# Transposing the exponentials of an attention block in two DMAs, high parts and low parts apart

## The chip, the cores and the metric

The kernel runs on one core of one Trainium2 chip. A core has a matrix engine (TensorE, in the profile PE, its weight loads PEld), a vector engine (VectorE, DVE), an activation engine (ScalarE, ACT), GpSimd (POOL), SyncE (SP, which here issues the DMAs) and 16 DMA engines that move what SP issues. The metric is the time of one execution on the device in microseconds (us); less is better.

## What is computed

Two request groups of 1024 rows and 1024 columns each go through the same two layers. Each layer is a hybrid block; the attention is the part that matters here.

```
h = rmsnorm(x) * (1 + scale) + shift          # from the conditioning vector
u = h @ w_in                                  # pool | q | k | v | rg | gate columns
y_pool, y_rg = pooling mixer, gated linear recurrence
q, k = rope(rmsnorm(q)), rope(rmsnorm(k))     # 8 query heads, 2 key heads, 64 wide
s = q @ k.T * scale;  p = softmax(s);  y_attn = p @ v
x = x + gate * rmsnorm((concat(y_pool, y_attn, y_rg) * silu(u_gate)) @ w_out)
```

## The kernel before

There are four passes (two layers times two groups, `n` = 0 to 3), one after the other with overlaps. Products are made of float16 numbers in pairs: an operand is split into a high part (rounded to float16) and a low part (the rest), and hi*hi, hi*lo and lo*hi are added in PSUM.

**The attention of one pass** (`attn_gen`, from line 1212) is 64 units, one for 128 query rows of one head. A unit goes through seven steps:

1. TensorE makes the scores of 128 rows against 1024 keys, four matmuls of 512 columns, into two PSUM banks.
2. VectorE finds the row maximum (`mx`).
3. ScalarE makes the exponentials (`p`), either in place in PSUM or into a buffer in SBUF, which frees the two banks sooner.
4. ScalarE rounds them to float16: the high part, `hh[:, 0, :]`.
5. GpSimd (exponentials in SBUF) or VectorE (in PSUM) subtracts it from the exponentials: the low part, `hh[:, 1, :]`.
6. One DMA transpose, 128 partitions by 2048 columns, turns both parts into `pT` (16 blocks of 128 by 128). The call is `dma_t` (line 478), and the profile has it under line 479.
7. TensorE multiplies `pT` with the values, 24 matmuls of 64 columns: 8 with the high parts against the high values, 8 with the low parts, and 8 with the high parts against the low values.

**What orders the work.** The whole program is laid out when it is built. Every piece of work is a generator that says what it needs, and the class `Order` (from line 84) keeps a clock of its own for each engine, for the DMA queue and for each tile, and takes the generator that can go on first, by rank where several can. Each engine then runs its instructions in the order so written; an instruction whose input isn't there holds all those behind it on its engine. All DMAs are issued by SP, in one order: the transposes, the loads of weights and rows, and the stores. `TUNE` (line 27) has some forty numbers for each pass: ranks of the pieces, how many units may be in flight (`nfly`), how many pairs of PSUM banks may hold scores (`np`), slacks in the choice of engine. `Order.dma` (line 242) books a transpose in that clock; `PARTS` and `keys` let the clock follow the pieces of a tile apart.

Buffers `p`, `hh` and `pT` come from a share of `nfly` + 2 slots of SBUF (`"u"`).

The end of a unit before, from line 1231 on:

```
hh = slot([P, 2, 1024], F16, "hh", "u")
...
act(hh[:, 0, :], p, AF.Copy)
...
tt(hh[:, 1, :], p, hh[:, 0, :], ALU.subtract)
free(p)
yield need("S", [hh], u=1)
pT = slot([P, 16, P], F16, "pT", "u")
dma_t(pT, hh.rearrange("p a s -> p (a s)"))
free(hh)
```

Of the kernel before, what the change touches and what calls it, by code (L numbers as in the profile page):

```python
# [10 lines left out]
F16 = mybir.dt.float16  # L11
# [5 lines left out]
P = 128  # L17
D = 1024
# [9 lines left out]


TUNE = [  # L30
    dict(h=-9.8, tab=-61.5, rgw=-62.8, qw=11.3, q=39.5, main=39.6, v=-93.1, rgt=6.2, attn=13.3,
         wprep=16.5, wo=39.7, side=108.5, gate=1.45, ysc=107.7, ysp=100.7, w=68.8, work=8, ds=3, nfly=8,
         s0=4, pace=(4, 61), wos=8, deep=3, f_major=5, spare=0, qkeep=1, wkeep=7, wokeep=0, slack=2.19,
         hslack=2.0, margin=0.33, P=0.6, A=1.22, D=1.02, G=1.25, S=1.3, X=2.99, nb=4, np=2, wopen=3,
         spill=2, sslack=0.0),
    dict(h=-88.0, tab=-138.2, rgw=-45.0, qw=-61.2, q=-181.1, main=65.6, v=-122.9, rgt=23.6, attn=-14.4,
         wprep=107.1, wo=85.3, side=97.8, gate=1.86, ysc=66.7, ysp=108.8, w=79.4, work=8, ds=2, nfly=5,
         s0=0, pace=(14, 64), wos=10, deep=3, f_major=6, spare=1, qkeep=5, wkeep=2, wokeep=9, slack=3.75,
         hslack=3.82, margin=0, P=0.07, A=1.29, D=0.36, G=1.39, S=1.66, X=1.74, nb=4, np=3, wopen=4,
         spill=2, sslack=0.0),  # L40
    dict(h=-56.5, tab=-120.9, rgw=-43.7, qw=-41.0, q=-17.5, main=-3.7, v=-95.2, rgt=51.8, attn=-16.0,
         wprep=71.4, wo=90.7, side=118.4, gate=0.1, ysc=142.5, ysp=110.2, w=62.9, work=6, ds=2, nfly=6,
         s0=3, pace=(15, 38), wos=9, deep=2, f_major=1, spare=4, qkeep=2, wkeep=0, wokeep=1, slack=2.33,
         hslack=2.48, margin=0.36, P=2.36, A=1.02, D=0.83, G=0.625, S=0.35, X=1.72, nb=6, np=2, wopen=3,
         spill=2, sslack=0),
    dict(h=-38.8, tab=-7.4, rgw=44.8, qw=-59.1, q=43.0, main=31.5, v=86.0, rgt=62.7, attn=36.1,
         wprep=226.9, wo=-31.1, side=118.1, gate=0.51, ysc=119.3, ysp=81.6, w=57.1, work=10, ds=3, nfly=5,
         s0=5, pace=(0, 64), wos=9, deep=4, f_major=3, spare=1, qkeep=5, wkeep=1, wokeep=0, slack=2.26,
         hslack=2.98, margin=0.87, P=0.28, A=0.15, D=0.45, G=0.9, S=1.99, X=0, nb=4, np=3, wopen=4,
         spill=2, sslack=0.28),  # L50
]
START = dict(x=(6, 16), xr=(-53.8009657012761, 1.4378218455368525), h=11.7, qw=-116.3, qw2=-141.6, qwa=9,
             prt=7, crow=4, prow=2, ada=95.9, keep=0)
LAYER = [
    dict(fly=6, keep=3, wfly=4, wfrom=(0, 0), wrank=15.7, ada=-17.0, akeep=5),
    dict(fly=3, keep=2, wfly=1, wfrom=(1, 1), wrank=163.6, ada=69.7, akeep=8),
]
LAT = {
# [6 lines left out]
PARTS = {}  # L65
# [8 lines left out]
def keys(ap):  # L74

    name = ap.name
    if name[:4] != "psum":
        step = PARTS.get(name)
        return (f"{name}/{ap.offset // step}",) if step else (name,)
    c = ap.offset % 4096  # L80
    return [f"psum/{i}" for i in range(c // 512, (c + sum(s * (n - 1) for s, n in list(ap.ap)[1:])) // 512 + 1)]
# [7 lines left out]
class Order:  # L89
# [18 lines left out]
    def spawn(self, rank, gen):  # L108
        insort(self.live, [rank, gen, None], key=lambda z: z[0])
# [132 lines left out]
    def dma(self, dur, outs, ins, hold, tail, e="S"):  # L242
        t = max(self.now, self.free_at[e], self.lanes[self.issued % 8])
        for ap in ins:
            t = max(t, self.there(ap.name, "S"))
        for ap in outs:
            t = max(t, self.last.get(ap.name, 0.0))
        x = max(t + 1.3, self.free_at["X"])
        self.free_at["X"] = x + dur
        self.free_at[e] = max(t + hold, x + dur - (1.8 if hold > 1.0 else 9.0))  # L250
        t = x + dur + tail
        self.lanes[self.issued % 8] = t
        self.issued += 1
        for ap in (*ins, *outs):
            self.last[ap.name] = max(self.last.get(ap.name, 0.0), t)
        for ap in outs:
            self.ready.setdefault(ap.name, {})["X"] = t

    def mark(self, name, *tiles):

# [40 lines left out]
def need(eng="", on=(), cond=None, keep=0, **bufs):  # L301
    return [eng, on, bufs, keep, cond, None]


def cols(ap):
    n = 1
    for x in ap.shape[1:]:
        n *= x
    return n
# [3 lines left out]
def tile_hymba_encoder(  # L313
# [43 lines left out]
    od = Order({"s": NS, "H": 2, "h": NH})  # L357
    free, spawn = od.free, od.spawn
# [3 lines left out]
    def nm(s):  # L362
        uid[0] += 1
        return f"{s}_{uid[0]}"

    def slot(shape, dt, name, pool="s"):
        return od.take(pool, sp.tile(shape, dt, tag="s", name=nm(name)))

    def half(shape, dt, name):
        return od.take("h", hp_.tile(shape, dt, tag="h", name=nm(name)))  # L370

    def small(n, name, dt=F32):
        return sm.tile([P, n], dt, tag="m", name=nm(name))

    def bank(name):
        i = od.bank(1)
        return banks[:, 512 * i:512 * i + 512]
# [99 lines left out]

    def dma_t(out, in_):
        nc.sync.dma_start_transpose(out=out, in_=in_)  # L479
        od.dma(2.55 * cols(in_) / 2048, [out], [in_], 1.8, 0.6)  # L480

    def soonest(*choice):

# [89 lines left out]
    G = {}  # L573

    def rows_dma(l, pr):
        for i, (r0, n, src) in enumerate((
# [9 lines left out]
        )):  # L586
            yield need("S", cond=lambda: l or G.get("adas", 0) >= START["prow"] + i)
            dma(pr[r0:r0 + n, :], src)

    def load_rows(l):  # L590
        yield need("S", h=1)
        pr = half([64, P], F32, "prow")
        yield from rows_dma(l, pr)
        yield need("P", [pr], b=1, cond=lambda: l or G.get("adas", 0) >= START["prt"])
        ps = bank("prT")
# [34 lines left out]
    def silu_c():  # L630
        yield need("S", h=1, cond=lambda: G.get("adas", 0) >= START["crow"])
        cr = half([16, P], F32, "crow")
# [196 lines left out]
    def h0_gen(rank):  # L829
# [4 lines left out]
        def load(j):  # L834
            yield need(s=8, cond=lambda: G.get("adas", 0) >= START["x"][j])
            xs = []
# [69 lines left out]
        spawn(-99.9, columns(0))  # L906
        spawn(START["xr"][0], load(0))
        spawn(START["xr"][1], load(1))
        yield need(cond=lambda: ("hgb", 0) in G)
# [250 lines left out]
    V16 = {}  # L1160
# [49 lines left out]
    def attn_gen(n, rank):  # L1210
        SUM, O, DONE = {}, {}, {}
        fly = [0]

        def unit(i, S):
            hp, q, e, t = UNITS[i]
            h = 2 * hp + e
            yield need("D", [S])
            mx = small(1, "mx")
            red(mx, S, ALU.max, negate=True)
            sc = G["qksc", n]  # L1220
            ts(mx, mx, sc, PSHIFT, ALU.mult, ALU.add)
            if (hp, q) not in SUM:
                SUM[hp, q] = sums.tile([P, 8], F32, tag="s8", name=nm("sum"))
            yield need("A", [mx], u=1)

            out = od.pairs >= TUNE[n]["spill"] and od.claims["u"] >= 2
            p = slot([P, 1024], F32, "p", "u") if out else S
            act(p, S, AF.Exp, bias=mx, scale=sc, accum=SUM[hp, q][:, 2 * t + e:2 * t + e + 1])
            if out:
                free(S)  # L1230
            hh = slot([P, 2, 1024], F16, "hh", "u")
            yield need("A", [p])
            act(hh[:, 0, :], p, AF.Copy)
            yield need("D", [hh])
            if out:
                sub_any(hh[:, 1, :], p, hh[:, 0, :])
            else:
                tt(hh[:, 1, :], p, hh[:, 0, :], ALU.subtract)
            free(p)
            yield need("S", [hh], u=1)  # L1240
            pT = slot([P, 16, P], F16, "pT", "u")
            dma_t(pT, hh.rearrange("p a s -> p (a s)"))
            free(hh)
            if (hp, q) not in O:
                yield need(b=1)
                if (hp, q) not in O:
                    O[hp, q] = bank("O")
                    DONE[hp, q] = 0
            yield need("P", [pT, V16[n, hp // 2]])
            v = V16[n, hp // 2]  # L1250
            c = (2 * t + e) * HD
            mms(O[hp, q][:, c:c + HD], [(pT[:, 8 * (a == 1) + st, :], v[:, st, HD * (a == 2):HD * (a == 2) + HD]) for a in range(3) for st in range(8)],
                True, True, (pT, v))
            free(pT)
            fly[0] -= 1
            if G["unit", n] == NU:
                held = sum(x == "u" for x in od.home.values())
                od.claims["u"] = max(0, min(od.claims["u"], fly[0] + 2 - held))
            DONE[hp, q] += 1
            if DONE[hp, q] == 8:  # L1260
                yield from join(hp, q)
# [29 lines left out]
        nfly = TUNE[n]["nfly"]  # L1291
        yield need(s=nfly + 2, cond=lambda: G.get(("rgc", n)) == 1 and G["side", n] >= TUNE[n]["s0"])
        od.claim("u", nfly + 2, True)
        for i in range(NU):
            hp, q, e, t = UNITS[i]
            h = 2 * hp + e
# [7 lines left out]
            S = bank2("S")  # L1304
# [523 lines left out]
```

## Time and profile before

| what | value |
|---|---|
| median of 3 runs | 1880.79 us (1875.88 to 1883.11) |
| the profiled execution, its own time | 1876.88 us |
| its span from first to last instruction | 1875.1 us |
| mean granted clock of TensorE, share of full speed | 0.975 |
| TensorE busy in matmuls | 1712.4 us (91% of the span) |
| VectorE, ScalarE, GpSimd busy | 1280.2, 1140.2, 760.5 us |
| bytes moved by DMAs | 323.58 MB |

The median says what the kernel takes. The profiled execution is one more run with the profiler on; its rows explain one another and its own time, so that sums are made against 1876.88 us and then held against the median.

Read the busy shares with care: an engine that is busy for 91% of the span leaves 9% for waits, and what can be gained at first is only in those waits. The profile names what ended each wait. SP has no busy time in the table, since all that it does is to wait and to issue; its rows (SPq) are instructions whose duration is the time that SP spent on the issue. A landing is the time from the start of that instruction until the last of its data is there.

### The profile page before, as it was taken

What the parts mean: (1) busy time and instruction counts of PE and PEld (TensorE: products, weight loads), DVE (VectorE), ACT (ScalarE), POOL (GpSimd) and SP (SyncE); (2) the same over time, 40 slices, a digit from 0 to 9 for tenths busy, and PEclk for the clock granted to TensorE, in tenths of its full rate; (3) what the DMA queues carried; (4) which work ended last, traced back from release to release, by engine and by line L of the source; (5) the groups of instructions that cost most, each with busy time, mean ns of one, the idle gap of its engine ahead of it and who ended that gap; (6) DMA issues with size and microseconds to landing.
All of it is one profiled execution on the core that took longest, in us unless ns stands there. A gap on an engine that the chain in (4) does not pass through costs nothing.

```text
span 1875.1 us, 35819 instructions
## 1 busy us (share of the span) xinstructions
PE 1712.4 (91%) x14267; PEld 990.7 (53%) x14267; DVE 1280.2 (68%) x2327; ACT 1140.2 (61%) x1767; POOL 760.5 (41%) x602
## 2 busy tenths in 40 slices
PE   5799899988999989999799998898789999999898
PEld 2564555544555546555456646455445755555543
DVE  4796987786345889567646689886843577866741
ACT  3665677776415667677642376678753256888721
POOL 2731452353431244234343226346643214655432
PEclk7899999999999989999899999999999999999999
DMA  9674499999365559999843446799984322999943
GB/s 345 201 208 153 99 191 233 178 214 252 136 225 191 131 137 206 168 194 214 232 147 135 101 102 128 145 251 191 179 234 151 102 68 41 178 201 195 198 133 116
DMA packets 672592, 323.58 MB, mean 173 GB/s; under 512 B 597880, under 2 KB 628776, under 8 KB 672424
## 3 DMA queue, kind: packets, MB, share of 16 engines
q1 hardware_dynamic: 672424, 321.29, 74.1%
q8 instruction: 111, 1.82, 0.4%
q14 instruction: 57, 0.47, 0.1%
HBM read 128.28 MB, written 46.15 MB: 93 GB/s over the span
## 4 chain that ended last, share of the span: by engine, by line
PE 32%; DVE 11%; issue 5%; ACT 4%; DMA 4%; POOL 4%; SPq 1%; POOLq 0%; ACTq 0%; DVEq 0%
PE psum L395 31%; POOL hh L423 4%; DMA pT<-hh 3%; DVE mx L459 3%; ACT p L410 2%; DVE psum L423 1%; ACT hh L410 1%; PE psum L403 1%; DVE y L450 1%; DMA xt<-xmid 1%; DVE sq L423 1%; SPq L479 1%; DVE hh L423 1%; DVE pdf L450 0%; DVE qss L459 0%
## 5 line engine op out<-in xcount | busy, mean ns | idle before, releaser
L423 POOL TENSOR_TENSOR hh<-p,hh 128x1024 f16<-128x1024 f32 x187 | 406.8, 2179 | 416.2 <-ACT hh L410 382.2
L395 PE MATMUL psum<-hT,w 128*128 128x512 f16 x2304 | 538.0, 381 | 5.8 <-ACT w L410 3.4
L459 DVE TENSOR_REDUCE mx<-psum 128x1 f32<-128x1024 f32 x256 | 312.0, 1219 | 94.2 <-PE psum L395 76.0
L395 PEld LDWEIGHTS <-w 128*128 128x128 f16 x2304 | 221.7, 99 | 273.6 <-issue 26.9
L395 PE MATMUL psum<-wo,y 128*128 128x512 f16 x1536 | 346.6, 382 | 3.7 <-DVE y L442 1.6
L395 PE MATMUL psum<-qkT,qkT 128*128 128x512 f16 x1024 | 265.7, 385 | 39.3 <-ACT p L410 24.7
L410 ACT ACTIVATE p<-psum,mx,qksc 128x1024 f32<-128x1024 f32 x187 | 224.1, 1199 | 106.8 <-DVE mx L444 63.9
L395 PE MATMUL psum<-w,hT 128*128 128x256 f16 x2304 | 273.5, 276 | 9.0 <-POOL hT L423 6.4
L395 PEld LDWEIGHTS <-pT 128*128 128x128 f16 x6144 | 212.8, 99 | 122.7 <-DMA pT<-hh 85.1
L395 PE MATMUL psum<-v,pT 128*128 128x64 f16 x6144 | 225.8, 194 | 54.8 <-DMA pT<-hh 54.6
L395 PEld LDWEIGHTS <-hT 128*128 128x128 f16 x2304 | 226.5, 100 | 60.3 <-issue 17.5
L395 PEld LDWEIGHTS <-y 128*128 128x128 f16 x1536 | 149.5, 99 | 175.4 <-issue 5.6
L410 ACT ACTIVATE hh<-p 128x1024 f16<-128x1024 f32 x187 | 196.5, 1053 | 4.9
L395 PEld LDWEIGHTS <-qkT 128*128 128x128 f16 x1024 | 93.0, 99 | 133.7 <-issue 58.0
L450 DVE SCALAR_TENSOR_TENSOR ot<-psum,ors,gp 128x512 f32<-128x512 f32 x64 | 45.1, 745 | 154.8 <-POOL ors L423 154.8
L410 ACT ACTIVATE junk<-psum 128x512 bf16<-128x512 f32 x64 | 38.2, 596 | 181.8 <-PE psum L395 170.4
L423 DVE TENSOR_TENSOR hh<-psum,hh 128x1024 f16<-128x1024 f32 x69 | 84.1, 1218 | 31.7 <-ACT hh L410 31.5
L423 POOL TENSOR_TENSOR ws<-ws,neghalf 128x1 f32<-128x1 f32 x46 | 28.5, 635 | 186.5 <-DVE ws L442 185.6
L423 POOL TENSOR_TENSOR ot<-ot,xres 128x1024 f32<-128x1024 f32 x31 | 73.2, 2361 | 66.7 <-DVE ot L450 32.5
L410 ACT ACTIVATE psum<-psum,mx,qksc 128x1024 f32<-128x1024 f32 x69 | 80.8, 1170 | 24.1 <-DVE mx L444 19.4
L410 ACT ACTIVATE hh<-psum 128x1024 f16<-128x1024 f32 x69 | 70.3, 1019 | 1.7
L423 POOL TENSOR_TENSOR qrs<-qrs,neghalf 128x8 f32<-128x8 f32 (+1 forms) x48 | 68.7, 1432 | 4.0
(219 smaller groups left out, 2073.1 us busy)
## 6 DMA issues: line engine op xcount, KB each, us to landing
adaw<-in_ada_w_dram SPq DMA_DIRECT2D x48, 512.0 KB, 6.1
wraw<-in_w_in_dram SPq DMA_DIRECT2D x36, 512.0 KB, 6.4
wd<-w SPq DMA_DIRECT2D x36, 512.0 KB, 3.3
w<-wd SPq DMA_DIRECT2D x36, 512.0 KB, 4.7
wo<-wd SPq DMA_DIRECT2D x32, 512.0 KB, 6.2
woraw<-in_w_out_dram SPq DMA_DIRECT2D x16, 512.0 KB, 4.6
wd<-wo SPq DMA_DIRECT2D x16, 512.0 KB, 4.1
xmid<-ot SPq DMA_DIRECT2D x16, 512.0 KB
```

The lines of the kernel that those rows point to most:

```text
L395: nc.tensor.matmul(out[:, :m], lhsT, rhs, start=start and i == 0, stop=stop and i == len(pairs) - 1)
L403: nc.tensor.transpose(out, in_, idn)
L410: nc.scalar.activation(out=out, in_=in_, func=func, **kw)
L423: eng.tensor_tensor(out=out, in0=a, in1=b, op=op)
L450: nc.vector.scalar_tensor_tensor(out=out, in0=a, scalar=s, in1=b, op0=op0, op1=op1)
L459: nc.vector.tensor_reduce(out=out, in_=a, op=op, **{"axis": AX.X, **kw})
L479: nc.sync.dma_start_transpose(out=out, in_=in_)
```

## The change

A unit now issues two transposes of 1024 columns instead of one of 2048. The first (`turn_hi`) is issued when the high part is there, and its slot for `pT` is taken then; the second follows when the low part is there, into the second half of the same `pT`. The matmuls with the values wait for both. `Order.dma` keeps the two halves of `hh` and `pT` apart and books each transpose at half the length. 26 numbers in the tables `TUNE`, `START` and `LAYER` are others (among them `np` of pass 0, 3 instead of 2, and ranks of the pieces `side`, `wo` and `attn`); of these one line of pass 0 and one of pass 3 stand here.

```diff
-         wprep=16.5, wo=39.7, side=108.5, gate=1.45, ysc=107.7, ysp=100.7, w=68.8, work=8, ds=3, nfly=8,
+         wprep=16.5, wo=43.7, side=158.1, gate=1.45, ysc=107.7, ysp=100.7, w=68.8, work=8, ds=3, nfly=8,
...
-         s0=5, pace=(0, 64), wos=9, deep=4, f_major=3, spare=1, qkeep=5, wkeep=1, wokeep=0, slack=2.26,
+         s0=5, pace=(0, 64), wos=9, deep=5, f_major=2, spare=1, qkeep=5, wkeep=1, wokeep=0, slack=2.26,
...
     def dma_t(out, in_):
         nc.sync.dma_start_transpose(out=out, in_=in_)
-        od.dma(2.55 * cols(in_) / 2048, [out], [in_], 1.8, 0.6)
+        od.dma(2.55 * cols(in_) / 2048, [out], [in_], 1.8 * cols(in_) / 2048, 0.6)
...
             hh = slot([P, 2, 1024], F16, "hh", "u")
+            PARTS[hh.name] = 1024
             yield need("A", [p])
             act(hh[:, 0, :], p, AF.Copy)
-            yield need("D", [hh])
+            got = []
+
+            def turn_hi():
+                yield need("S", [hh[:, 0, :]], u=1)
+                pT = slot([P, 16, P], F16, "pT", "u")
+                PARTS[pT.name] = 1024
+                dma_t(pT[:, :8, :], hh[:, 0, :])
+                got.append(pT)
+
+            spawn(rank, turn_hi())
+            yield need("D", [hh[:, 0, :]])
             if out:
                 sub_any(hh[:, 1, :], p, hh[:, 0, :])
             else:
                 tt(hh[:, 1, :], p, hh[:, 0, :], ALU.subtract)
             free(p)
-            yield need("S", [hh], u=1)
-            pT = slot([P, 16, P], F16, "pT", "u")
-            dma_t(pT, hh.rearrange("p a s -> p (a s)"))
+            yield need(cond=lambda: got)
+            pT = got[0]
+            yield need("S", [hh[:, 1, :]])
+            dma_t(pT[:, 8:, :], hh[:, 1, :])
             free(hh)
...
-            yield need("P", [pT, V16[n, hp // 2]])
+            yield need("P", [pT[:, :8], pT[:, 8:], V16[n, hp // 2]])
```

The engines' work stays nearly the same: TensorE has the same instructions in another order, SP has 936 DMAs instead of 680 (512 transposes of `pT` instead of 256). Of the 256 subtractions of a low part VectorE makes 75 instead of 69 and GpSimd 181 instead of 187; of 48 copies of `hT` VectorE makes 15 instead of 6 and ScalarE 33 instead of 42.

What SP issues in the middle of the attention of pass 0, before (`pT` and `hh` with the numbers of their buffers; `wo` and `wd` are halves of the output projection's weights that come back from DRAM, or go there):

```order
L471 DMA wo_3282<-wd_848 128x2048
L479 DMA_TRANSPOSE pT_3296<-hh_3227 128x16x128
L471 DMA wo_3349<-wd_881 128x2048
L471 DMA wo_3385<-wd_943 128x2048
L471 DMA wd_3394<-w_3142 128x2048
L479 DMA_TRANSPOSE pT_3401<-hh_3294 128x16x128
L479 DMA_TRANSPOSE pT_3446<-hh_3383 128x16x128
L471 DMA wo_3469<-wd_976 128x2048
L471 DMA wo_3483<-wd_1062 128x2048
L471 DMA wo_3520<-wd_1081 128x2048
L479 DMA_TRANSPOSE pT_3522<-hh_3462 128x16x128
```

and now, at the load from the same `wd_976`:

```order
L473 DMA wo_3566<-wd_976 128x2048
L481 DMA_TRANSPOSE pT_3574<-hh_3518 128x8x128
L481 DMA_TRANSPOSE pT_3551<-hh_3509 128x8x128
L481 DMA_TRANSPOSE pT_3624<-hh_3534 128x8x128
L481 DMA_TRANSPOSE pT_3574<-hh_3518 128x8x128
L481 DMA_TRANSPOSE pT_3644<-hh_3565 128x8x128
L481 DMA_TRANSPOSE pT_3624<-hh_3534 128x8x128
L481 DMA_TRANSPOSE pT_3683<-hh_3591 128x8x128
L481 DMA_TRANSPOSE pT_3644<-hh_3565 128x8x128
L481 DMA_TRANSPOSE pT_3683<-hh_3591 128x8x128
L481 DMA_TRANSPOSE pT_3742<-hh_3648 128x8x128 x2
L481 DMA_TRANSPOSE pT_3782<-hh_3677 128x8x128 x2
```

The first mention of a `pT` is its high half, the second its low half. In the upper rows the high half of the next unit stands ahead of the low half of this one; in the last two (x2) both halves of a unit follow each other. Of the 256 units 123 are of that second kind. The eight loads of `wo` stood within 15 rows of SP's order (five of them above); now they are spread over 44.

What SP issues at the end of the attention of pass 0, before (`xt` are rows of the other group, `gp` the gate row of the residual add):

```order
L471 DMA xt_4975<-in_x_sample_dram 128x1024
L479 DMA_TRANSPOSE pT_4979<-hh_4886 128x16x128
L471 DMA xt_5013<-in_x_sample_dram 128x1024
L479 DMA_TRANSPOSE pT_5025<-hh_4899 128x16x128
L471 DMA gp_5034<-gscr_1876 128x1024
L479 DMA_TRANSPOSE pT_5063<-hh_4935 128x16x128
L471 DMA xt_5107<-in_x_sample_dram 128x1024
L471 DMA xt_5116<-in_x_sample_dram 128x1024
L479 DMA_TRANSPOSE pT_5148<-hh_4970 128x16x128
```

and now, down to the last transpose of that attention and past it:

```order
L481 DMA_TRANSPOSE pT_5136<-hh_5120 128x8x128 x2
L481 DMA_TRANSPOSE pT_5174<-hh_5134 128x8x128
L473 DMA xt_5184<-in_x_sample_dram 128x1024
L481 DMA_TRANSPOSE pT_5174<-hh_5134 128x8x128
L481 DMA_TRANSPOSE pT_5218<-hh_5178 128x8x128 x2
L481 DMA_TRANSPOSE pT_5232<-hh_5222 128x8x128 x2
L473 DMA xt_5293<-in_x_sample_dram 128x1024
L473 DMA gp_5298<-gscr_1876 128x1024
L473 DMA xt_5314<-in_x_sample_dram 128x1024
```

One `xt` stands between the last transposes instead of four `xt` and `gp`; the others come behind them.

## Rows read from the trace of the kernel before

**Rows 1.** The page: span, busy time, share of the span, instructions of each engine.

```profile
span 1875.1 us, 35819 instructions
...
PE 1712.4 (91%) x14267; PEld 990.7 (53%) x14267; DVE 1280.2 (68%) x2327; ACT 1140.2 (61%) x1767; POOL 760.5 (41%) x602
```

**Rows 2.** The waits of TensorE: who waited for whom, us, times, longest.

```profile
PE psum L395 <- DMA pT<-hh: 54.6, 49, 4.3
PE psum L395 <- ACT p L410: 28.5, 30, 2.9
PE psum L403 <- DMA crow<-in_c_sample_dram: 10.0, 1, 10.0
```

**Rows 3.** The four attentions as windows: length, busy (instructions) by engine, PEclk, DMA share, GB/s.

```profile
209.00:458.00 249.00, 220.94 (x2390) 131.54 (x2389) 199.99 (x322) 186.78 (x274) 112.11 (x66) 0.98 1.02 197
649.00:916.00 267.00, 238.70 (x2441) 140.69 (x2440) 198.46 (x317) 191.69 (x275) 108.07 (x68) 0.96 0.96 192
1106.00:1385.00 279.00, 243.75 (x2469) 142.66 (x2467) 219.14 (x349) 192.10 (x280) 143.88 (x79) 0.98 0.90 185
1588.00:1805.00 217.00, 203.28 (x2274) 118.69 (x2272) 161.57 (x244) 163.32 (x236) 108.68 (x55) 1.00 1.03 189
sum 1012.00, PE 906.66 PEld 533.58 DVE 779.15 ACT 733.88 POOL 472.75; mean PE 226.67 PEld 133.40 DVE 194.79 ACT 183.47 POOL 118.19
```

**Rows 4.** The tile hh: durations in ns, least, median, most, first and last start.

```profile
L479 SPq DMA_TRANSPOSE pT<-hh x256: 1616/2504/5682, 198.4 to 1790.4; - x128
L410 ACT ACTIVATE hh<-p x187: 1039/1057/1087, 192.7 to 1783.5; 128x1024 f16<-128x1024 f32 x187
L423 POOL TENSOR_TENSOR hh<-p,hh x187: 2122/2130/3110, 193.8 to 1784.6; 128x1024 f16<-128x1024 f32 x187
L410 ACT ACTIVATE hh<-psum x69: 1002/1022/1033, 216.0 to 1784.4; 128x1024 f16<-128x1024 f32 x69
L423 DVE TENSOR_TENSOR hh<-psum,hh x69: 1208/1216/1226, 219.5 to 1787.4; 128x1024 f16<-128x1024 f32 x69
...
DMA to landing us min/median/max: 4.3/5.0/8.2
```

**Rows 5.** SP in order of time, 296 to 331 us: start, us, what.

```profile
299.17 4.90 SPq L479 DMA_TRANSPOSE pT<-hh  x1
304.17 1.00 SPq L471 DMA_DIRECT2D wo<-wd  x2
305.26 0.38 SPq L471 DMA_DIRECT2D wd<-w  x1
305.74 7.68 SPq L479 DMA_TRANSPOSE pT<-hh  x2
313.51 1.99 SPq L471 DMA_DIRECT2D wo<-wd  x3
315.59 10.30 SPq L479 DMA_TRANSPOSE pT<-hh  x3
```

**Rows 6.** The waits of SP itself over the span: us, times, longest.

```profile
SPq L479 <- POOL hh L423: 280.6, 101, 39.4
...
SPq L479 <- DVE hh L423: 44.1, 8, 21.0
```

**Rows 7.** The tile rgraw, loads of 32 KB: SP's durations and the landings.

```profile
L471 SPq DMA_DIRECT2D rgraw<-in_rg_wa_dram x16: 596/605/732, 48.7 to 1417.1; - x16
...
DMA to landing us min/median/max: 2.1/2.2/3.3
```

**Rows 8.** The waits of TensorE in 395 to 450 us, the end of pass 0's attention.

```profile
PE psum L395 <- DMA pT<-hh: 9.1, 8, 3.6
```

**Rows 9.** The waits of TensorE in 880 to 916 us, the end of pass 1's attention.

```profile
PE psum L395 <- DMA pT<-hh: 9.5, 5, 4.3
```

**Rows 10.** SP in order of time, 430 to 456 us.

```profile
446.33 2.61 SPq L471 DMA_DIRECT2D rgraw<-in_rg_wa_dram  x4
448.98 2.56 SPq L471 DMA_DIRECT2D rgraw<-in_rg_wx_dram  x4
```

More of the change, by code (lines that the diff above doesn't have):

```diff
@@ L30 @@
 TUNE = [
-    dict(h=-9.8, tab=-61.5, rgw=-62.8, qw=11.3, q=39.5, main=39.6, v=-93.1, rgt=6.2, attn=13.3,
-         wprep=16.5, wo=39.7, side=108.5, gate=1.45, ysc=107.7, ysp=100.7, w=68.8, work=8, ds=3, nfly=8,
+    dict(h=-9.8, tab=-61.5, rgw=-62.8, qw=15.8, q=39.5, main=39.6, v=-93.1, rgt=6.2, attn=13.3,
+         wprep=16.5, wo=43.7, side=158.1, gate=1.45, ysc=107.7, ysp=100.7, w=68.8, work=8, ds=3, nfly=8,
          s0=4, pace=(4, 61), wos=8, deep=3, f_major=5, spare=0, qkeep=1, wkeep=7, wokeep=0, slack=2.19,
-         hslack=2.0, margin=0.33, P=0.6, A=1.22, D=1.02, G=1.25, S=1.3, X=2.99, nb=4, np=2, wopen=3,
+         hslack=2.0, margin=0.33, P=0.6, A=1.22, D=1.02, G=1.25, S=1.3, X=2.99, nb=4, np=3, wopen=3,
@@ L35 @@
          spill=2, sslack=0.0),
[L36 to L39, printed above, removed]
+    dict(h=-88.0, tab=-138.2, rgw=-45.0, qw=-61.2, q=-181.1, main=65.6, v=-122.9, rgt=23.6, attn=16.6,
+         wprep=107.1, wo=90.2, side=97.8, gate=3.08, ysc=66.7, ysp=108.8, w=79.4, work=8, ds=2, nfly=5,
+         s0=0, pace=(14, 64), wos=10, deep=3, f_major=5, spare=1, qkeep=5, wkeep=2, wokeep=9, slack=3.75,
+         hslack=3.82, margin=0, P=0.07, A=1.29, D=0.36, G=1.26, S=1.66, X=1.74, nb=4, np=3, wopen=4,
@@ L40 @@
          spill=2, sslack=0.0),
     dict(h=-56.5, tab=-120.9, rgw=-43.7, qw=-41.0, q=-17.5, main=-3.7, v=-95.2, rgt=51.8, attn=-16.0,
[L42 to L47, printed above, removed]
-         s0=5, pace=(0, 64), wos=9, deep=4, f_major=3, spare=1, qkeep=5, wkeep=1, wokeep=0, slack=2.26,
+         wprep=71.4, wo=90.7, side=122.0, gate=0.1, ysc=142.5, ysp=110.2, w=62.9, work=6, ds=3, nfly=6,
@@ new lines @@
+         s0=3, pace=(15, 38), wos=9, deep=2, f_major=1, spare=4, qkeep=0, wkeep=0, wokeep=1, slack=2.33,
+         hslack=2.48, margin=0.36, P=2.36, A=1.02, D=0.83, G=0.24, S=0.35, X=1.72, nb=6, np=2, wopen=3,
+         spill=2, sslack=0.05),
+    dict(h=-38.8, tab=-7.4, rgw=44.8, qw=-59.1, q=41.8, main=31.5, v=86.0, rgt=78.7, attn=36.1,
+         wprep=226.0, wo=-30.1, side=118.1, gate=0.51, ysc=119.3, ysp=94.6, w=57.1, work=8, ds=3, nfly=5,
+         s0=5, pace=(0, 64), wos=9, deep=5, f_major=2, spare=1, qkeep=5, wkeep=1, wokeep=0, slack=2.26,
@@ L49 @@
          hslack=2.98, margin=0.87, P=0.28, A=0.15, D=0.45, G=0.9, S=1.99, X=0, nb=4, np=3, wopen=4,
-         spill=2, sslack=0.28),
+         spill=2, sslack=0.69),
 ]
-START = dict(x=(6, 16), xr=(-53.8009657012761, 1.4378218455368525), h=11.7, qw=-116.3, qw2=-141.6, qwa=9,
-             prt=7, crow=4, prow=2, ada=95.9, keep=0)
+START = dict(x=(6, 16), xr=(-53.8009657012761, 1.4378218455368525), h=11.7, qw=-118.9, qw2=-141.6, qwa=9,
+             prt=5, crow=4, prow=2, ada=95.9, keep=0)
 LAYER = [
-    dict(fly=6, keep=3, wfly=4, wfrom=(0, 0), wrank=15.7, ada=-17.0, akeep=5),
+    dict(fly=6, keep=3, wfly=4, wfrom=(0, 0), wrank=15.7, ada=-17.0, akeep=6),
@@ L244, in dma @@
         for ap in ins:
-            t = max(t, self.there(ap.name, "S"))
+            t = max(t, max(self.there(n, "S") for n in keys(ap)))
         for ap in outs:
-            t = max(t, self.last.get(ap.name, 0.0))
+            t = max(t, max(self.last.get(n, 0.0) for n in keys(ap)))
         x = max(t + 1.3, self.free_at["X"])
         self.free_at["X"] = x + dur
-        self.free_at[e] = max(t + hold, x + dur - (1.8 if hold > 1.0 else 9.0))
+        self.free_at[e] = max(t + hold, x + dur - (1.8 if hold > 0.7 else 9.0))
         t = x + dur + tail
@@ L254, in dma @@
         for ap in (*ins, *outs):
-            self.last[ap.name] = max(self.last.get(ap.name, 0.0), t)
+            for n in (ap.name, *keys(ap)):
+                self.last[n] = max(self.last.get(n, 0.0), t)
         for ap in outs:
-            self.ready.setdefault(ap.name, {})["X"] = t
+            for n in (ap.name, *keys(ap)):
+                self.ready.setdefault(n, {})["X"] = t
     def mark(self, name, *tiles):
@@ L1252, in unit @@
             mms(O[hp, q][:, c:c + HD], [(pT[:, 8 * (a == 1) + st, :], v[:, st, HD * (a == 2):HD * (a == 2) + HD]) for a in range(3) for st in range(8)],
-                True, True, (pT, v))
+                True, True, (pT[:, :8], pT[:, 8:], v))
             free(pT)
```

## The prediction

> **What bounds the kernel now.** I read the busy table first. TensorE works 1712.4 of 1875.1 us, the next engine, VectorE, 1280.2 [rows 1]. So no engine's work has to shrink for the time to fall, and none of it does; what can be won lies in TensorE's 163 idle microseconds, and the question is who causes them. The waits of TensorE answer that [rows 2]: the largest entry is the transposed exponentials, 54.6 us in 49 waits with a longest of 4.3; then 28.5 us for PSUM banks that ScalarE has not yet emptied (`ACT p`); the first load, 10.0 us once, has nothing to do with this change.
>
> Next I ask why `pT` is late. The four attentions are 1012 us of the span, and in them the DMA engines are busy at shares of 0.90 to 1.03, where packets overlap, so that the sum passes 1 [rows 3]. SP spends 2504 ns in the median on one transpose of `pT` [rows 4]; 256 of them are 641 us, 63% of those 1012 us. In a stretch such as 299 to 326 us SP issues without a pause: a transpose from 299.17 for 4.90 us, the next DMA at 304.17, 0.10 us later [rows 5]. There a transpose is late because others are before it in the queue. Elsewhere SP itself stands still: 280.6 us in 101 waits for GpSimd's low part and 44.1 us in 8 for VectorE's [rows 6]. So the queue has both: idle time while it waits for a low part, and a backlog once that part is there. A unit hands in its 2048 columns only at the end of the subtraction, though half of them were ready 2130 ns earlier on GpSimd, 1216 ns on VectorE [rows 4].
>
> **The change, part by part.**
>
> *The low half has less to move.* The trace has no transpose of 1024 columns, so I bound its landing. Above: a whole one lands 4.3 us after issue at the least [rows 4]. Below: a load of 32 KB lands in 2.1 us [rows 7], which is about what a DMA costs apart from its bytes. If the difference goes with the columns, a half lands in 3.2 us (an estimate from those two rows), so a unit whose low half finds the queue free is complete 1.1 us earlier. The ends are 0 and 2.2 us. The high half is hidden: it has 2.1 us of GpSimd's subtraction for its transfer. Where the exponentials stay in PSUM, VectorE's 1.2 us cover about half of it.
>
> *What that takes from TensorE's waits.* Of the 54.6 us, 9.1 in 8 waits lie at the end of pass 0's attention [rows 8] and 9.5 in 5 at the end of pass 1's [rows 9], where units are transposed close together and little other work for TensorE is left. The remaining 36 us in 36 waits are 1.0 us each in the mean, about what a half saves. The ends of this term are 0 (the queue is behind in all of them, and the high halves only queue up) and 36 (all gone). I take two thirds, **24 us off**: SP's idle time [rows 6] is six times as long as these waits, so that there is room for most high halves before the backlog, but a part of the waits follows stretches without any room [rows 5].
>
> *The end of pass 0's attention.* By the order, four loads of `xt` and one of `gp` stood between its last transposes, and one `xt` stands there now. Its 9.1 us [rows 8] have 0 and 9.1 as ends; I take half, **4 us off**. For the end of pass 1 I take nothing, since its last units come close together as before and a queue of transposes stays a queue.
>
> *What 256 further DMAs cost the queue.* Their bytes are the same, so only the price of one more issue counts. Below: 0, if the halves run into each other. Above: 0.65 us, what SP took for each of the eight loads of 32 KB (2.61 and 2.56 us for four) [rows 10]. The nearest row is a transpose itself, behind which SP goes on after 0.10 us [rows 5]; I take that. Most of it falls into SP's idle time. Where TensorE still waits it counts: the worst landing of 8.2 us is 3.9 above the least [rows 4], some one and a half transposes of 2.5 us, say two, and with the late one itself three further issues, 0.3 us. After the first term 12 of the 36 waits are left and the 13 of the ends, 25 in all: **7 us on**.
>
> Here the Trainium skill speaks against the change. Its page "DMA: Bandwidth & Descriptors", section "Rules for kernel authors", says that many small transfers should be joined into one large one, and this change does the reverse. The same page, section "Anatomy of one DMA — SWDGE (gpsimd) path", gives a fixed part of some 2.0 us to a DMA issued from GpSimd; if 256 further ones paid that one after the other, it would be 512 us, an estimate from that page. Its own account of that part is mostly waiting for the landing, and the loads of 32 KB show it overlapped [rows 7, 10]: 0.65 us from issue to issue, 2.1 us to land.
>
> *Engines.* Six subtractions move from GpSimd to VectorE, 6 times 1.216 us, under VectorE's 233 idle microseconds in the attentions (1012 less 779.15) [rows 3, 4]: nothing. If that cover were gone it would cost 7 us. The nine copies that move to VectorE are of the same order, and I leave them at nothing too.
>
> *Slots.* `pT` takes its slot some 2.1 us earlier. Units come every 4 us (1012 by 256), so this holds half a slot more of the `nfly` + 2: the six units whose exponentials now stay in PSUM are what it costs. Where it costs more, that shows as a longer wait for `ACT p`.
>
> *The 26 numbers.* They lay out the same work in another order. `np` of pass 0 allows one more pair of PSUM banks for scores, which aims at the 28.5 us of `ACT p` [rows 2]; exponentials that stay in PSUM work against it. The ends are 28.5 us off and as much on, if twice as many scores wait; I take 0.
>
> **The sum.** 1876.9 - 24 - 4 + 7 = 1855.9, so **1856 us**, 1.1% under the profiled execution. That execution is itself 3.9 us under the median of the runs, 1880.79; I make no correction for it.
>
> **The rivals.**
>
> *The queue stays the bound (no change).* SP issues in one order and holds everything behind the DMA that waits. In 123 of 256 units both halves stand next to each other there, and between them SP waits for GpSimd with the next unit's high half behind it. If the waits of TensorE follow only stretches like that of 299 to 326 us [rows 5], the halves move the same bytes at the same time, the first term is 0, and what is left is -4 + 7: 1880 us. For it speaks the DMA share near 1 in three of four attentions [rows 3]; against it the 280.6 us in which the queue had nothing to do [rows 6]. That the change doesn't do what it says, sending the high half early, would look the same and is counted here.
>
> *The issue becomes the price (slower).* If a transpose costs SP a fixed time whatever its length, the queue loses it 256 times. It decides at 0.35 us each: three further issues then eat the 1.05 us that a half gains. At 0.65 us [rows 10] every one of the 49 waits grows by 3 times 0.65 less 1.05, 0.9 us, in all +44, or 1921 us; at 0.5 us, halfway, by 0.45, in all +22, or 1899 us. The place is SP's queue in such stretches [rows 5]. For it speaks that the small loads show such a price and that the queue has little room. Against it: the shortest whole transpose takes SP 1616 ns [rows 4], less than the 2504 ns that the queue leaves between them, so that twice the fixed part may still fit under the transfer. The Trainium skill's rule on joining transfers is this rival's.
>
> *More than the waits shrinks (faster).* If the ends and `ACT p` go as well, the floor is 1876.9 - 54.6 - 28.5 = 1794; halfway between this and the forecast is 1825 us. For it speaks that TensorE has other work to fill with; against it that ScalarE, VectorE and the queue are all busy over 70% of the attentions [rows 3].
>
> **How the numbers follow.** The forecast has 0.50, the unchanged queue 0.24, the price of issues 0.17, the larger gain 0.09. A measurement of this kernel tells about 0.5% from no change, 9.4 us: below 1871.4 is faster, above 1890.2 slower. So faster 0.59, same 0.24, slower 0.17. The range goes from 1826, with half of the larger gain left out below, to 1894, with the middle and upper part of the slower rival left out above; together that leaves out some 0.18. Both ends lie inside the bounds of the terms.
>
> **What would show it.** In the profile of the changed kernel: 512 transposes of `pT` with SP's median near 1.25 us and a least landing near 3.2 us (the first step). TensorE's waits for `pT` near 54.6 - 24 - 4 + 7, 34 us, with the end of pass 0's attention at about half. If the median of SP's transposes is above 1.6 us, so that two take longer than the 2.5 of one and 0.35 on each, the slower rival has it. If SP's waits for GpSimd stay at 280 us and TensorE's for `pT` above 45 us, the queue was the bound. The prediction is wrong in its root if `pT` waits fall as said and the time doesn't: then `ACT p`, or a wait that is not among the largest now [rows 2], has taken the place.

## The result: slower by 1.4%, outside the forecast range

| | before | with the change |
|---|---|---|
| median | 1878.34 us (1873.29 to 1883.11, 4 runs) | 1905.33 us (1899.71 to 1908.68, 4 runs) |
| ratio | | 1.0141, 95% interval 1.0101 to 1.0181 |
| profiled execution, its span | 1876.88, 1875.1 us | 1907.24, 1905.3 us |
| mean granted clock of TensorE in it | 0.975 | 0.962 |

The forecast was 1856 us, with a range of 1826 to 1894.

The page of the changed kernel, the line of busy times (against [rows 1]):

```profile
span 1905.3 us, 36502 instructions
...
PE 1736.2 (91%) x14267; PEld 1009.5 (53%) x14267; DVE 1283.3 (67%) x2343; ACT 1133.2 (59%) x1757; POOL 756.8 (40%) x598
```

TensorE has the same 14267 matmuls and is busy 23.8 us longer; it is idle for 169.1 us (1905.3 less 1736.2) instead of 162.7. So in this pair of executions 24 of the 30 us are time in which TensorE counts as busy with the same matmuls, and 6 are waits. Most of the 24, 17.9 us, are the matmuls with the values (busy us, mean ns, idle before; before, then with the change):

```profile
L395 PE MATMUL psum<-v,pT 128*128 128x64 f16 x6144 | 225.8, 194 | 54.8 <-DMA pT<-hh 54.6
```

```profile
L397 PE MATMUL psum<-v,pT 128*128 128x64 f16 x6144 | 243.7, 197 | 77.6 <-DMA pT<-hh 76.7
```

The clock has a share in that, but not all: e4 below has the clock of before, 0.975, and 237.0 us there. Besides, the pair overstates the clock: over the timed runs it was 0.964 to 0.978 before (23 runs beside the experiments) and 0.962 to 0.972 after (four). The medians differ by 0.003 (0.971 and 0.968), which is some 6 us of 1905 if all time went with the clock (an estimate).

The waits of TensorE (against [rows 2]):

```profile
PE psum L397 <- DMA pT<-hh: 76.7, 64, 5.0
PE psum L397 <- ACT p L412: 18.1, 23, 2.1
```

The waits for `pT`, which were to fall from 54.6 to about 34 us, rose to 76.7. Those for `ACT p` fell by 10.4 us.

The tile `hh` (against [rows 4]) and two of SP's own waits for it (against [rows 6]; us, times, longest):

```profile
L481 SPq DMA_TRANSPOSE pT<-hh x512: 1231/1283/3806, 196.3 to 1810.9; - x171
```

```profile
SPq L481 <- ACT hh L412: 110.5, 79, 13.0
SPq L481 <- ACT p L412: 72.1, 44, 9.4
...
SPq L481 <- POOL hh L425: 64.7, 61, 4.3
```

A half takes SP 1283 ns in the median, as foreseen. SP now waits 64.7 us for GpSimd's low parts instead of 280.6; but it waits 182.6 us (the first two lines) for ScalarE, which makes the high parts. So much of the idle time has only moved ahead of the high half. Nor is the fall from 280.6 a sign of the early issue: e4 and e5 below, which issue both halves at one place, have 70.2 and 69.1 us for GpSimd as well.

### The profile page after: what moved, and what is told of

The parts are those of the page before. It is cut to its first block, busy times and chain, and to the rows that moved or that the text cites. A ratio compares the mean times of both kernels' runs of the same rounds, so it can differ in the third digit from the quotient of the medians.

```text
span 1905.3 us, 36502 instructions
## 1 busy us (share of the span) xinstructions
PE 1736.2 (91%) x14267; PEld 1009.5 (53%) x14267; DVE 1283.3 (67%) x2343; ACT 1133.2 (59%) x1757; POOL 756.8 (40%) x598
## 5 line engine op out<-in xcount | busy, mean ns | idle before, releaser
L425 POOL TENSOR_TENSOR hh<-p,hh 128x1024 f16<-128x1024 f32 x181 | 393.7, 2179 | 404.8 <-ACT hh L412 395.8
L397 PE MATMUL psum<-v,pT 128*128 128x64 f16 x6144 | 243.7, 197 | 77.6 <-DMA pT<-hh 76.7
L397 PEld LDWEIGHTS <-pT 128*128 128x128 f16 x6144 | 227.8, 101 | 142.6 <-DMA pT<-hh 89.1
L412 ACT ACTIVATE p<-psum,mx,qksc 128x1024 f32<-128x1024 f32 x181 | 217.1, 1200 | 122.7 <-DVE mx L446 60.1
L412 ACT ACTIVATE hh<-p 128x1024 f16<-128x1024 f32 x181 | 189.9, 1053 | 4.7
L412 ACT ACTIVATE psum<-psum,mx,qksc 128x1024 f32<-128x1024 f32 x75 | 87.9, 1172 | 34.1 <-DVE mx L446 33.9
L425 DVE TENSOR_TENSOR hh<-psum,hh 128x1024 f16<-128x1024 f32 x75 | 91.3, 1218 | 21.0 <-ACT hh L412 20.6
L446 POOL TENSOR_SCALAR qrs<-qss,wu 128x8 f32<-128x8 f32 (+1 forms) x48 | 13.1, 273 | 161.9 <-DVE qss L461 160.7
L412 ACT ACTIVATE hh<-psum 128x1024 f16<-128x1024 f32 x75 | 76.5, 1021 | 1.0
```

What stands on the lines that cost most here:

```text
L397: nc.tensor.matmul(out[:, :m], lhsT, rhs, start=start and i == 0, stop=stop and i == len(pairs) - 1)
L412: nc.scalar.activation(out=out, in_=in_, func=func, **kw)
L425: eng.tensor_tensor(out=out, in0=a, in1=b, op=op)
L446: eng.tensor_scalar(out=out, in0=a, scalar1=s1, scalar2=s2, op0=op0, op1=op1)
```

## The experiments

Each run was laid against theories that say where the loss comes from. Theory P: the price of 256 further issues is the loss. Theory O: the order of the work is. From the second group on two more are asked: F, that the order of before fits the chip unusually well and any other is slower; M, that the new order is bad because a half is booked too short. T says that the split is good and the new order bad, S that an early half does harm by itself, B that SP blocks its queue with high halves whose copies aren't done.

| run | order laid out with | transposes | median us | ratio to before, interval |
|---|---|---|---|---|
| e1 | split, numbers of before | halves, high early | 1922.79 | 1.0236 (1.0211 to 1.0262) |
| e2 | whole, numbers of the change | whole | 1910.93 | 1.0174 (1.0148 to 1.0201) |
| e3 | order of the change | whole | 1907.91 | 1.0155 (1.0124 to 1.0186) |
| e4 | order of before | both halves late | 1887.85 | 1.0056 (1.0036 to 1.0076) |
| e5 | order of the change | both halves late | 1908.52 | 1.0150 (1.0135 to 1.0165) |
| e6 | order of before | halves, high at its copy | 1909.53 | 1.0153 (1.0136 to 1.0170) |
| e7 | before, 2.56 booked | whole | 1903.54 | 1.0127 (1.0112 to 1.0142) |
| e8 | change, 1.37 a half booked | halves, high early | 1918.26 | 1.0205 (1.0190 to 1.0221) |
| e9 | order of before | halves, high at the subtraction | 1891.25 | 1.0062 (1.0043 to 1.0081) |
| e10 | before, 2.54 booked | whole | 1892.51 | 1.0064 (1.0042 to 1.0086) |
| e11 | change, 2.56 booked | halves, high early | 1909.76 | 1.0160 (1.0143 to 1.0177) |
| e12 | change, 2.54 booked | halves, high early | 1917.97 | 1.0205 (1.0185 to 1.0225) |

Before was run beside each group of four: 1879.59, 1879.62 and 1880.08 us.

### The code and the numbers apart: e1, e2

e1 has the split with the tables of before (one line of its edit, against the change), e2 the whole transpose with the tables of the change:

```diff
-         wprep=16.5, wo=43.7, side=158.1, gate=1.45, ysc=107.7, ysp=100.7, w=68.8, work=8, ds=3, nfly=8,
+         wprep=16.5, wo=39.7, side=108.5, gate=1.45, ysc=107.7, ysp=100.7, w=68.8, work=8, ds=3, nfly=8,
...
```

> The two half transposes, with the 26 numbers of before. Theory P (price of the issue): SP spends 1.28 us and a pause of 0.09 on a half, 2.74 us a unit instead of some 2.5, so the queue is the loss and the numbers are not: about 1905 us, as slow as the change. Theory O (order): the new numbers lay TensorE's work out worse and the split itself costs nothing: 1860 to 1880 us.

> One whole transpose as before, laid out anew with the 26 numbers of the change. Theory P: no dearer issue, so about the 1878 us of before, give or take 10. Theory O: the numbers are the loss, about 1905 us.

Measured: 1922.79 and 1910.93. Neither edit alone is faster than both together. P misses e2, which has no further issues and loses 31 us; O misses e1, where the old numbers with the split lose most. Neither part alone explains the loss; what both runs share with the change is an order that is new.

### The same order, other transposes: e3, e4, e5

Here the layout's clock books what it booked, so that TensorE, VectorE, ScalarE and GpSimd run their instructions in an unchanged order; `dma_t` is given what SP really issues. e3 in the order of the change:

```diff
-                dma_t(pT[:, :8, :], hh[:, 0, :])
+                dma_t(pT[:, :8, :], hh[:, 0, :], [])
...
-            dma_t(pT[:, 8:, :], hh[:, 1, :])
+            dma_t(pT[:, 8:, :], hh[:, 1, :], [(pT, hh.rearrange("p a s -> p (a s)"))])
```

e5 issues both halves there, `[(pT[:, :8, :], hh[:, 0, :]), (pT[:, 8:, :], hh[:, 1, :])]`, and e4 the same two in the order of before, where the whole one stood.

> TensorE, VectorE, ScalarE and GpSimd run in exactly the order of the change; SP issues one whole transpose where the low half's stood, and nothing where the high half's stood. Theory P: the 256 issues saved are worth more than the early start: 1880 us. Theory O: the order is built on an early high half, and a whole transpose lands 1.1 us later: 1905 to 1935 us.

> The order of before on all engines; where SP issued a whole transpose it now issues its two halves one behind the other, so nothing starts earlier and only the issues are added. Theory P: 0.24 us a unit and a later low half: 1895 to 1910 us. Theory O: the price of an issue is small beside SP's waits: 1878 to 1888 us.

> The order of the change on all four engines; both halves are issued at the low half's place, so nothing starts early. If 256 issues cost what they cost in the old order (8 us) and the early high half wins back some 11, this stands 8 us above the run with whole transposes in this order: 1916 us. If the early high half is worth nothing, it is as fast as the change: 1905 us.

Measured: e3 1907.91, e4 1887.85, e5 1908.52. e3 is the run that decides. It has the very transposes of before and no further issue, and it is as slow as the change: the order costs 28 us without any split. (Order means here also where buffers are taken. It was laid out for an early high half, which e3 lacks; the change has it, and is within 3 us.) e4 costs 8 us by the medians, 7 to 14 by the interval. In the order of the change the three ways to transpose stand within 4 us of each other (1907.91, 1908.52, 1905.33) with intervals that overlap, so the early high half is worth nothing that these runs can tell, and neither the issues nor the early start can be read there.

e4 is not the bare price of the issues. TensorE's waits for `pT` are 52.5 us in it, not more than the 54.6 of before, and its idle time is the same (161.4 against 162.7 us). What grew, at the same clock of 0.975, is the busy time of the matmuls with the values, by 11.2 us:

```profile
L395 PE MATMUL psum<-v,pT 128*128 128x64 f16 x6144 | 237.0, 195 | 52.9 <-DMA pT<-hh 52.5
```

They are now often done in two goes, 8 with the high half and 16 when the low half is there; what that costs is seen in a stretch of the change below. And against what was expected of e4 and e5, something does start earlier in them: where SP stood waiting for a low part, it now issues the high half first, as its own waits in e4 show:

```profile
SPq L480 <- ACT hh L410: 96.1, 78, 19.5
...
SPq L480 <- POOL hh L423: 70.2, 62, 5.6
SPq L480 <- ACT p L410: 58.2, 39, 9.4
```

So e4 is the price of the halves less what that gains. Two halves that are both held until the low part is there were not run.

The tile `pT` in e4 gives a half's landing, least, median, most:

```profile
L480 SPq DMA_TRANSPOSE pT<-hh x512: 1232/1287/4087, 198.8 to 1798.8; - x171
...
DMA to landing us min/median/max: 3.1/3.8/7.4
```

### Where the order loses: behind two attentions, and at the end of pass 2's

Cut into stages by the ends of the attentions, 23 of the 30 us lie in two stretches (length, then busy of PE, PEld, DVE, ACT, POOL with instructions; PEclk, DMA share, GB/s). Behind pass 0's attention and behind the last one, before:

```profile
458.00:650.00 192.00, 189.67 (x1141) 103.38 (x1140) 104.71 (x243) 83.31 (x151) 57.50 (x67) 1.00 0.56 182
...
1805.00:1876.00 71.00, 62.13 (x288) 27.99 (x286) 12.67 (x18) 11.00 (x32) 24.40 (x31) 0.98 0.32 112
```

With the change:

```profile
455.00:659.00 204.00, 198.34 (x1168) 107.39 (x1167) 113.79 (x251) 84.89 (x157) 58.24 (x69) 1.00 0.53 173
...
1824.00:1906.00 82.00, 73.31 (x340) 33.06 (x338) 12.66 (x18) 11.01 (x32) 24.41 (x31) 0.96 0.29 102
```

TensorE does more there. Its matmuls of the output projection in the last attention (1588 to 1805 us) and behind it, before:

```profile
L395 PE MATMUL psum<-wo,y 128*128 128x512 f16 x97 | 22.2, 379 | 0.8 <-POOL y L423 0.8
```

```profile
L395 PE MATMUL psum<-wo,y 128*128 128x512 f16 x288 | 62.3, 379 | 0.0
```

With the change (1610 to 1824 us, and behind):

```profile
L397 PE MATMUL psum<-wo,y 128*128 128x512 f16 x46 | 11.7, 413 | 0.0
```

```profile
L397 PE MATMUL psum<-wo,y 128*128 128x512 f16 x340 | 73.5, 379 | 0.0
```

51 of them no longer fill the attention, which is only 3 us shorter for it (214 instead of 217), and 52 more stand behind it, where they cost their full time. Pass 0 has the same: 45 instead of 84 in its attention, which takes 247 instead of 249 us, and 341 instead of 301 behind it. e3 has it with whole transposes: 81 us behind the last attention, with 334 such matmuls, and 200 behind pass 0's.

In pass 2, whose attention takes 285 us instead of 279 [rows 3], the filling is used up too early. The last 119 us of that attention, before, with the change and in e3: first the window, then TensorE's groups in it (busy us, mean ns, idle before and what ended it).

Before:

```profile
1266.00:1385.00 119.00, 96.39 (x1153) 56.11 (x1152) 79.55 (x108) 83.45 (x120) 66.64 (x34) 0.97 1.04 205
```

```profile
L395 PE MATMUL psum<-qkT,qkT 128*128 128x512 f16 x120 | 31.7, 389 | 9.6 <-ACT p L410 9.4
L395 PE MATMUL psum<-v,pT 128*128 128x64 f16 x840 | 30.9, 195 | 8.4 <-DMA pT<-hh 8.4
L395 PE MATMUL psum<-wo,y 128*128 128x512 f16 x95 | 23.9, 397 | 2.5 <-DVE y L442 1.6 <-ACT p L410 0.6 <-DVE y L450 0.3
L395 PE MATMUL psum<-hT,w 128*128 128x512 f16 x76 | 18.5, 379 | 0.0
```

With the change:

```profile
1290.00:1409.00 119.00, 86.19 (x1085) 54.33 (x1083) 80.41 (x111) 88.97 (x124) 67.06 (x42) 0.91 1.05 206
```

```profile
L397 PE MATMUL psum<-v,pT 128*128 128x64 f16 x840 | 36.9, 203 | 27.3 <-DMA pT<-hh 27.3
L397 PE MATMUL psum<-qkT,qkT 128*128 128x512 f16 x121 | 35.2, 418 | 3.0 <-ACT p L412 2.2 <-DVE otmp L425 0.6
L397 PE MATMUL psum<-wo,y 128*128 128x512 f16 x82 | 19.0, 379 | 0.0
...
L397 PE MATMUL psum<-hT,w 128*128 128x512 f16 x12 | 2.9, 379 | 0.0
```

e3, the order of the change with whole transposes:

```profile
1284.00:1403.00 119.00, 86.88 (x1083) 53.49 (x1082) 82.64 (x112) 88.92 (x124) 66.69 (x41) 0.90 1.00 210
```

```profile
L397 PE MATMUL psum<-v,pT 128*128 128x64 f16 x840 | 35.0, 204 | 23.9 <-DMA pT<-hh 23.8
```

In all three TensorE does the same attention (840 matmuls with the values, 120 or 121 for scores). Before, 171 projection matmuls stand between them (95 and 76), with the change 94 (82 and 12). Most of the others stand earlier in the same attention: 379 matmuls of `hT` with `w` come ahead of these 119 us, instead of 309. I read it so: attention without such filling runs at the pace of the queue, whose DMA share is about 1 in all three, and TensorE is idle for 32.8 us instead of 22.6, while the clock is 0.91 instead of 0.97. e3 shows the same with whole transposes, 32.1 us and 0.90.

What such a stretch looks like with the change, TensorE in order of time from 1330 us (start, us, what, idle before):

```profile
1330.42 0.40 PE L397 MATMUL psum<-v,pT 128*128 128x64 f16 x8
1334.49 1.03 PE L397 MATMUL psum<-v,pT 128*128 128x64 f16 x16 [3.67 <-DMA pT<-hh]
1335.33 1.90 PE L397 MATMUL psum<-qkT,qkT 128*128 128x512 f16 x4
...
1345.20 0.40 PE L397 MATMUL psum<-v,pT 128*128 128x64 f16 x8
1348.11 0.64 PE L397 MATMUL psum<-v,pT 128*128 128x64 f16 x16 [2.51 <-DMA pT<-hh]
1348.59 1.03 PE L397 MATMUL psum<-qkT,qkT 128*128 128x512 f16 x4
...
1354.20 0.86 PE L397 MATMUL psum<-v,pT 128*128 128x64 f16 x24
```

and SP at the same time:

```profile
1328.37 0.52 SPq L473 DMA_DIRECT2D xt<-xmid  x1
1328.94 12.77 SPq L481 DMA_TRANSPOSE pT<-hh  x7
```

The early half is there: TensorE does its first eight matmuls at 1330.42. Then it stands for 3.67 us in the middle of the 24 until the low half has landed, and SP issues without a pause behind a load of `xt`. To have half of the operand early is worth 0.4 us here. (In the layout's clock the matmuls with the values wait for both halves; on the chip the first eight wait for the high one alone.) The eight that take the high half against the low values stand behind those with the low half in the code, so they could not go ahead; the other order of the three groups was not tried. And two goes have a price: 0.40 and 0.64 us from 1345.20 on, 1.04 in all, against 0.86 for the 24 in one at 1354.20.

### How much any other order costs: e7, e10, e8, e11, e12

e7 and e10 change only the length that the layout's clock books for a transpose in the kernel before, by 10 ns; e11 and e12 do the same to the change; e8 books a half as its profile has it:

```diff
-        od.dma(2.55 * cols(in_) / 2048, [out], [in_], 1.8, 0.6)
+        od.dma(2.56 * cols(in_) / 2048, [out], [in_], 1.8, 0.6)
```

```diff
-        od.dma(2.55 * cols(in_) / 2048, [out], [in_], 1.8 * cols(in_) / 2048, 0.6)
+        od.dma(2.55 * cols(in_) / 2048 if cols(in_) > 1024 else 1.37, [out], [in_], 1.8 if cols(in_) > 1024 else 1.28, 0.6)
```

> The kernel before; only the length that the layout's clock books for a transpose is 2.56 instead of 2.55 us, which says the same of the chip but makes another order. Theory F (the order of before was a lucky fit to the chip, any other is slower): 1895 to 1925 us. Theory M (the order of the change is bad because it books a half too short): 1874 to 1886 us.

> The change; the layout's clock books a half as measured in its profile, 1.37 us of the queue and 1.28 us of SP, instead of 1.275 and 0.9. Theory M (booked too short): 1875 to 1890 us. Theory F: another order like any, 1895 to 1925 us.

> The kernel before with a transpose booked at 2.54 instead of 2.55 us: a third order with whole transposes that wasn't chosen on the chip. Theory F (the order of before is the exception): 1895 to 1915 us. Against it: 1872 to 1888 us.

> The change with 2.56 instead of 2.55 us booked for 2048 columns: another order with halves. Theory F with a split that is worth nothing: about as the disturbed orders with whole transposes, 1900 to 1920 us. If the change's own order was chosen well, it lies above the 1905 us of the change.

> The same with 2.54: one more order with halves, 1900 to 1920 us by theory F. A time under 1885 us would say that the split is good and that the change had a poor order by chance.

Measured: 1903.54, 1918.26, 1892.51, 1909.76, 1917.97. Ten nanoseconds in the booking, which say nothing new of the chip, cost the kernel before 24 and 12 us. The change gets 13 us slower by them in e12, and by no more than the intervals allow in e11. e10 came out faster than F had it. M falls: with the measured price booked the change gets 13 us slower. The waits of TensorE in e7 show that the waits for `pT` are not what such an order loses by:

```profile
PE psum L395 <- DMA pT<-hh: 42.9, 42, 4.0
PE psum L395 <- ACT p L410: 17.9, 15, 2.2
PE psum L395 <- DVE hh L423: 15.4, 12, 3.8
```

Both of the large entries of [rows 2] are smaller than before, and it is 24 us slower: others took their place, such as the 15.4 us for the subtraction on VectorE, and its attention of pass 0 takes 261 us instead of 249. Orders with halves that nothing was fitted to (e1, e8, e11, e12) stand at 1909.76 to 1922.79, those with whole transposes (e2, e7, e10) at 1892.51 to 1910.93. That fits a split that costs something, but so few orders that scatter by 18 us show no more than that.

### The early half in the order of before: e6, e9

e6 issues the high half as soon as its copy is laid out; e9 only where the subtraction is laid out. The order of the four engines is that of before; the buffer of `pT` is taken that much earlier, outside the layout's books.

```diff
             act(hh[:, 0, :], p, AF.Copy)
+            pT = sp.tile([P, 16, P], F16, tag="s", name=nm("pT"))
+            nc.sync.dma_start_transpose(out=pT[:, :8, :], in_=hh[:, 0, :])
```

> The order of before on all four engines; the high half is transposed as soon as its copy is made, the low half where the whole transpose stood. Theory T (the split is good, the new order is bad): 11 us under the old order with both halves late, 1868 to 1878 us. Theory S (the split is bad by itself): SP stands behind halves whose inputs are late, 1890 us or more.

> The order of before on all four engines; the high half is issued where the subtraction is laid out, so later than in the run with the early high half, when its copy should be done. Theory B (there SP blocked the queue with copies that were not done): most of the loss goes, 1878 to 1890 us, and below 1887 if an early high half is worth anything. Theory S (an early half is harmful by itself): 1900 to 1910 us.

Measured: 1909.53 and 1891.25. T falls. The waits of SP in e6 point to its loss:

```profile
SPq L1236 <- ACT p L410: 140.2, 68, 20.8
SPq L1236 <- ACT hh L410: 92.0, 59, 18.3
```

SP waits 232 us for ScalarE in front of high halves (line 1236), with the low halves and loads of others behind it. In e9 the same two are 103.6 and 86.0 us, in e4 they were 58.2 and 96.1, and the times follow: in e9 18 of the 30 us are gone. That speaks for B, though e9 stands just above the 1878 to 1890 us that B had, and since e9 also takes the buffer of `pT` later than e6, the blocked queue and the longer held buffer aren't told apart. e9 is no faster than e4, where high halves go ahead only of a low part that SP would have waited for (intervals 1.0043 to 1.0081 and 1.0036 to 1.0076). In this order too, a still earlier start pays for nothing that can be told.

## Why the prediction was wrong

- **"The 26 numbers ... I take 0" failed, and that is as much as the change loses.** The order that the layout makes with the change costs 28 us with whole transposes (e3); the change loses 27. That is the bad end of the 28.5 that I had bounded the term with for another reason. I treated the order as neutral because the work was the same. It isn't the numbers alone, either: the old ones with the split (e1) and the new ones without (e2) are no faster, and 10 ns of booking (e7, e10) are enough for 12 to 24 us. The order of before is better than every other order tried here, so each new layout of this program started with a loss. The 49 us between forecast and result are about these 28, with the 24 and 4 us of the next terms that weren't gained, less the 7 for issues, which this order doesn't show (e5 against e3, 0.6 us).
- **"What that takes from TensorE's waits", 24 us off, failed.** The half lands 1.2 us earlier, as said (3.1 us at the least in e4 against 4.3), but TensorE's waits for `pT` rose by 22 us, and with the order fixed the earlier issue gains nothing that can be told (the change against e5, e9 against e4). I argued from SP's idle time [rows 6] that there was room for the high halves ahead of the backlog. But SP's idle time moved in front of the high half, and the long waits of TensorE that were looked at lie in stretches where SP issues without a pause. The rival of the queue had this term right; its time, 1880 us, missed the order as mine did.
- **"What 256 further DMAs cost", 7 us on, came out in number, 8 us in e4, but not in its working.** It was to be 0.3 us on each of 25 waits; in e4 the waits for `pT` don't grow, and what grows is the busy time of the matmuls with the values, done in two goes. That the number fits is luck.
- **"The end of pass 0's attention", 4 us off, held in its place only.** TensorE's waits for `pT` in 395 to 455 us are now 0.9 us in 2; they were 9.1 [rows 8]. The stretch behind it is 12 us longer. The end of pass 1 has 9.5 us in 5 as before [rows 9], as taken.
- **Engines and slots** stand as taken: VectorE 1283.3 us instead of 1280.2, and `ACT p` fell rather than rose.
- **The slower rival came out near the time (1899) for the wrong reason.** Its fixed price was to be 0.5 us an issue; the signs named for it are absent (SP's median is 1283 ns, under 1.6 us), and the halves cost 8 us of the 27 in the order of before, and nothing that can be told in the order of the change. The rule of the Trainium skill's page "DMA: Bandwidth & Descriptors", section "Rules for kernel authors", to join small transfers, agrees with e4 in its direction, by 0.6%.

What stays open: why the layout puts less filling into the attentions or uses it up earlier in the new order, what the halves and the early issue are each worth alone, and whether some order with halves beats 1880 us. None of the nine runs with halves did; they have six orders, and e4, e6 and e9 that of before.

## What to carry to other kernels

Where a program is laid out by a planner, an edit is two edits: the operation, and a new order of everything. Price the operation with the order held fixed, and measure how far the time moves when the planner is disturbed by something that means nothing; here that was 12 to 24 us, against 8 us for the operation. An early start of half a transfer was worth nothing here that could be told: the consumer could go on with that half for 0.4 us, and then waited for the other half behind the same queue. So ask first how far the consumer gets with the half, and what stands in the queue ahead of the rest.

## What the runs showed of the hardware

- **A transpose of half the columns takes SP more than half the time**: 1231 ns at the least (the line of `hh` above) against 1616 for the whole [rows 4]. If the rest goes with the columns, 2 x 1231 - 1616, some 850 ns of each are fixed (an estimate), more than the 0.65 us that I had as the upper end for one further issue. In the median it hardly shows: two halves take SP 2 x 1283 ns, 62 ns more than the 2504 of a whole one [rows 4].
- **One stop of TensorE was paid twice.** Three windows of the changed kernel, next to each other, in the columns above:

```profile
1327.00:1334.00 7.00, 2.45 (x40) 1.85 (x40) 6.80 (x6) 5.01 (x8) 4.93 (x2) 0.93 1.04 189
1334.00:1344.00 10.00, 8.61 (x99) 6.05 (x100) 8.52 (x11) 9.55 (x14) 6.17 (x4) 0.54 0.86 177
1344.00:1355.00 11.00, 6.17 (x92) 3.89 (x91) 7.83 (x11) 10.91 (x16) 8.85 (x6) 1.00 1.07 193
```

  TensorE works 2.45 of 7 us, and then the granted clock is 0.54 of 2.4 GHz, nearly all of it the level of 1.2. The four score matmuls take 1.90 us at 1335.33 and 1.03 at 1348.59, when the clock is back. Not every thin stretch goes that way: in the third window TensorE works 6.17 of 11 us at 1.00.
